# Probabilities of token tiles 4 to 7 transposed on VectorE in 32x32 blocks and moved to their rows by DMA; leftover keys on VectorE too; opening reordered

## The chip, the cores and the metric

One core of one Trainium2 chip runs the whole kernel. The metric is the device time of one launch in microseconds (us); lower is better.

## The reference, cut to what matters

One layer of a hybrid model over 1024 tokens with 16 learned meta tokens in front (L = 1040), width 1024, all in float32. One input projection feeds three mixers (a short convolution, an attention with 8 heads, a retention); their gated outputs are joined and go through an output projection that is added to the input. The change concerns the attention:

```python
cid = jnp.where(pos < 16, 0, 1 + (pos - 16) // 64)       # chunks of 64 keys, 16 meta keys in front
s = jnp.einsum('bqhd,bkhd->bhqk', qb, k) * scale         # qb: one block of 128 queries
s = jnp.where(cid_keys <= cid_queries, s, neg)
p = jax.nn.softmax(s, axis=-1)
o = jnp.einsum('bhqk,bkhd->bqhd', p, v)
o = o.reshape(B, Lp, 512) * jax.nn.silu(z)               # z: gate from the input projection ("mz")
...
h = h + y @ w_out
```

## The kernel before, in words

Matrix products keep float32 accuracy by splitting each operand in a high and a low part; `mm3` (lines 109 to 112) then issues three matmuls for one product. The kernel has three stretches.

**Opening** (0 to about 60 us). After eight warm-up matmuls, the unit `mz` of the input projection is computed from input tiles and weights that arrive by DMA. Lines 217 to 243 load the rows of x, square and sum them, and multiply a diagonal matrix on TensorE to spread the row factors (`rps`, L243). Then `rest` computes the remaining columns of `mz`, a loop over four blocks b gates and stores them (`mz_s`, L260), and unit A follows with weights `ws_A`, whose later tiles are loaded on the SP queue behind L260's stores.

**Projections, convolution and retention** (to about 345 us). Nothing of it is changed.

**Attention** (about 345 to 531 us): 8 heads of 8 token tiles t of 128 queries. A loop over n = 8h + t (lines 835 to 864) writes the work in this order: `score` of the tile that lies LA = 4 ahead, `p_t` of tile n, the transposes `qk_t` of the queries and keys of head h + 2 at tiles 3, 3, 4 and 4 (table `QK`), `attend` one tile after the last of its group of four, and `partial`, matmuls of the output projection for the mixers that are done, by a table of due tiles.
- `score` (L681 to 711): matmuls S of queries on 16 + 128(t + 1) keys into one of two PSUM slots (tile 7 needs two, S_7_0 and S_7_2); VectorE takes the row maximum (L693), ScalarE the exponential with its sum (L702) into a buffer `pr`, VectorE the reciprocal (L708); GpSimd scales the last 16 keys into `pm` (L710) and the rest in place (L711). There are 5 `pr` buffers (3 + LA - 2), taken in turn.
- `p_t` (L714 to 742): TensorE transposes `pr` in blocks of 128 keys (L724) into PSUM `pTp`, and ScalarE (L730) or, for blocks from 4 on, VectorE (L728) copies them to `pt`. The 16 leftover keys of four tiles are transposed together from `pm` (`mTp`, L736) and copied in four pieces to `ptm` (VectorE L740, ScalarE L742).
- `attend` (L744 to 773): matmuls of v on `pt` into PSUM tile `o` (L765), with the leftover keys last (L767), and two multiplications with the gate in `ym` (L773, VectorE).
- `qk_t` (L662 to 677): four transposes for 512 queries or keys (`qTp`, `kTp`), then ScalarE writes the high part, VectorE the low part.

`kTp`, `qTp` and `o` share one PSUM bank ("x"): each must be emptied before the next may start. S has two slots, `pTp` two, `part` one.

The order of instructions on each engine is fixed when the kernel is built, by a scheduler that simulates a timeline; priorities come from the order in which the code is written. At run time each engine follows its list and waits at the first instruction whose inputs are not there.

## Time and profile before

| | before |
|---|---|
| median of 3 runs | 580.92 us (580.18 to 584.61) |
| the profiled execution's own time | 581.55 us |
| span in its profile | 579.8 us |
| TensorE busy | 569.8 us, 98% |
| VectorE / ScalarE / GpSimd busy | 330.9 / 255.0 / 224.1 us |
| granted TensorE clock | 1.00 throughout (2.4 GHz) |
| chain that ended last | TensorE 83%, DMA 9%, VectorE 3% |

Each figure is one profiled execution. Busy times are sums over instructions; matmuls are pipelined, so that several of them lie over one another and a mean per matmul is longer than the time that one more of them takes. The chain of work that ended last has no such overlap: its pieces follow one another.

### The profile page before, as it was taken

Reading aid. Unit: us, or ns where it says so; the run is one execution under the profiler, and the core shown is the slowest. Engines: PE = TensorE matmul, PEld = TensorE weight load, DVE = VectorE, ACT = ScalarE, POOL = GpSimd, SP = SyncE. Lnnn points to the kernel's source line nnn. Section 1 sums busy time; section 2 is a strip of 40 time slices with the busy share of each in tenths; the row PEclk is TensorE's granted clock in tenths of the full one; section 3 lists DMA queues with packets and bytes.
Section 4 is the critical chain, followed back from the end, with each engine's and each line's share of the span. In section 5 each row is a group of like instructions: output and inputs, shape, how many; then the busy total and the mean of one; then the engine's idle time right before and its main releaser. Section 6 shows DMA issues by size and latency. Waiting matters only on the chain.

```text
span 579.8 us, 9595 instructions
## 1 busy us (share of the span) xinstructions
PE 569.8 (98%) x3401; PEld 481.7 (83%) x3401; DVE 330.9 (57%) x761; ACT 255.0 (44%) x616; POOL 224.1 (39%) x330
## 2 busy tenths in 40 slices
PE   8999999999999999999999999999999999999997
PEld 5877899988888888898898888898888888876886
DVE  5547768888536432553332667675757857664132
ACT  6765535665234332532010438475655646543000
POOL 2023258677103220151242968443524334624000
PEclk9999999999999999999999999999999999999999
DMA  8887513274703200130030648235112223113096
GB/s 326 289 265 241 182 67 120 108 224 158 234 1 92 74 0 19 54 110 18 20 97 1 199 145 273 73 103 171 56 38 73 77 71 128 37 68 116 1 301 224
DMA packets 46657, 70.39 MB, mean 121 GB/s; under 512 B 3792, under 2 KB 21840, under 8 KB 46480
## 3 DMA queue, kind: packets, MB, share of 16 engines
q1 hardware_dynamic: 43008, 63.47, 33.8%
q10 hardware_dynamic: 3600, 6.29, 2.9%
q8 instruction: 27, 0.44, 0.3%
q14 instruction: 22, 0.18, 0.1%
HBM read 48.75 MB, written 21.00 MB: 120 GB/s over the span
## 4 chain that ended last, share of the span: by engine, by line
PE 83%; DMA 9%; DVE 3%; ACT 2%; issue 2%; POOL 0%; SPq 0%; DVEq 0%; ACTq 0%; POOLq 0%
PE r L112 16%; PE S L112 9%; PE cv L112 8%; PE part L112 7%; PE A L112 6%; PE o L765 6%; PE pTp L724 5%; PE cz L112 4%; PE cb L112 4%; DMA out<-ot 4%; PE out L112 3%; PE qps L112 3%; DMA xs<-in_xT 2%; DMA xt<-in_x 2%; PE rsp L477 1%
## 5 line engine op out<-in xcount | busy, mean ns | idle before, releaser
L702 ACT ACTIVATE pr<-S,smx 128x144 f32<-128x144 f32 (+8 forms) x72 | 50.4, 701 | 27.3 <-DVE smx L693 13.4
L693 DVE TENSOR_REDUCE smx<-S 128x1 f32<-128x144 f32 (+8 forms) x72 | 49.8, 701 | 15.7 <-PE S L112 6.3
L710 POOL TENSOR_SCALAR pm<-pr,smx 128x16 f32<-128x16 f32 x64 | 18.4, 288 | 85.2 <-DVE smx L708 61.3
L711 POOL TENSOR_SCALAR pr<-pr,smx 128x128 f32<-128x128 f32 (+3 forms) x64 | 48.1, 752 | 0.6 <-DVE smx L708 0.6
L724 PE MATMUL pTp<-ident,pr 128*128 128x128 f32 x288 | 45.4, 274 | 1.5 <-ACT pt L730 1.4
L730 ACT COPY pt<-pTp 128x512 f32<-128x512 f32 (+2 forms) x64 | 31.8, 505 | 26.3 <-PE pTp L724 24.9
L451 POOL TENSOR_SCALAR kw<-qk,con 128x64 f32<-128x64 f32 (+1 forms) x36 | 13.8, 397 | 71.7 <-DVE qk L447 58.4
L724 PEld LDWEIGHTS pTp<-ident,pr 128*128 128x128 f32 x288 | 35.0, 140 | 7.0 <-POOL wol L104 1.8
L765 PEld LDWEIGHTS o<-pt,v 128*64 128x64 f32 x448 | 26.5, 137 | 12.1 <-issue 4.7
L765 PE MATMUL o<-pt,v 128*64 128x256 f32 (+2 forms) x448 | 36.2, 309 | 0.0
L112 PE MATMUL r<-wh_r,xal 128*128 128x512 f32 (+1 forms) x80 | 30.5, 381 | 0.0
L112 PE MATMUL r<-wh_r,xah 128*128 128x512 f32 (+1 forms) x80 | 30.4, 380 | 0.0
L112 PE MATMUL part<-woh,yh 128*128 128x512 f32 x64 | 30.1, 470 | 0.0
L112 PE MATMUL r<-wl_r,xah 128*128 128x512 f32 (+1 forms) x80 | 30.0, 375 | 0.0
L882 DVE SCALAR_TENSOR_TENSOR ot<-out,xr 128x512 f32<-128x512 f32 (+1 forms) x17 | 11.2, 660 | 31.1 <-DMA out<-ot 16.8
L112 PE MATMUL r<-wl_r,xbh 128*128 128x512 f32 x64 | 26.1, 409 | 0.0
L112 PE MATMUL r<-wh_r,xbh 128*128 128x512 f32 x64 | 25.7, 401 | 0.0
L112 PE MATMUL part<-wol,yh 128*128 128x512 f32 x64 | 25.5, 399 | 0.0
L112 PE MATMUL r<-wh_r,xbl 128*128 128x512 f32 x64 | 25.5, 398 | 0.0
L112 PE MATMUL part<-woh,yl 128*128 128x512 f32 x64 | 25.2, 394 | 0.0
L773 DVE TENSOR_TENSOR ym<-o,ym 64x256 f32<-64x256 f32 x32 | 13.5, 421 | 16.7 <-PE o L767 16.2
L104 POOL TENSOR_TENSOR wol<-wos,woh 128x512 fp32r<-128x512 f32 x16 | 20.4, 1291 | 2.6 <-ACT woh L103 2.6
(295 smaller groups left out, 1716.1 us busy)
## 6 DMA issues: line engine op xcount, KB each, us to landing
xt<-in_x SPq DMA_DIRECT2D x16, 256.0 KB, 4.5
ws_r<-in_win SPq DMA_DIRECT2D x16, 256.0 KB, 3.3
ws_c<-in_win SPq DMA_DIRECT2D x16, 256.0 KB, 2.9
wos<-in_wout SPq DMA_DIRECT2D x16, 256.0 KB, 3.8
xp<-in_x SPq DMA_DIRECT2D x16, 256.0 KB, 2.7
p_s<-xp SPq DMA_DIRECT2D x16, 256.0 KB, 2.0
xr<-p_s SPq DMA_DIRECT2D x15, 256.0 KB, 4.5
out<-ot ACTq DMA_DIRECT2D x15, 256.0 KB, 4.5
```

Of the source, the lines that this page charges most:

```text
L104: (lo_eng or nc.vector).tensor_tensor(lo, src, hi.bitcast(F32), op=ALU.subtract)
L112: nc.tensor.matmul(out, lhsT=x_, rhs=y_, start=first and i == 0, stop=last and i == 2)
L451: nc.gpsimd.tensor_scalar(kw[R, j], qk[R, 2 + j], con[R, kd0 + j:kd0 + j + 1], 1.0, op0=ALU.mult, op1=ALU.mult)
L693: nc.vector.tensor_reduce(sm[:, i // 2:i // 2 + 1], sp[:, :n, :w], axis=AX.XY, op=ALU.max, negate=True)
L702: e = nc.scalar.activation(pr[:, c0:c1].rearrange("p (b c) -> p b c", b=n), sp, AF.Exp, bias=mx, accum_out=sm[:, 5 + i:6 + i])
L710: nc.gpsimd.tensor_scalar(pm[(2 * h + t // 4) % 2][:, t % 4, :NM], pr[:, nk - NM:nk], sm[:, 9:10], 1.0, op0=ALU.mult, op1=ALU.mult)
L711: nc.gpsimd.tensor_scalar(pr[:, :nk - NM], pr[:, :nk - NM], sm[:, 9:10], 1.0, op0=ALU.mult, op1=ALU.mult)
L724: tr_ = nc.tensor.transpose(out=tp[:, b * P:b * P + P], in_=pr[:, c0:c0 + P], identity=ident)
L730: nc.scalar.copy(pt[:, b0:b0 + nb, tt], src)
L765: nc.tensor.matmul(op[64 * cg:64 * cg + 64, c0:c1], lhsT=lv, rhs=src[:, i_, c_], start=b == 0, stop=False)
L773: nc.vector.tensor_tensor(ys, op[64 * cg:64 * cg + 64, :256].rearrange("p (a c q) -> p a c q", a=2, q=64), ys, op=ALU.mult)
L882: nc.vector.scalar_tensor_tensor(ot, acc[:, c0:c1], 0.5, xt, op0=ALU.mult, op1=ALU.add)
```

## The change

1. **Tiles 4 to 7.** Their `pr` is no longer transposed on TensorE. VectorE transposes it within 32x32 blocks (L737 of the changed kernel) into a buffer `td`, and 16 DMAs for each pair of tiles (L746, on the SP queue, 32 partitions with rows of 352 or 480 elements) move the blocks to the partitions on which their keys belong, in `pt`. That is 32 DMAs per head, 256 in all. Tiles 0 to 3 are transposed on TensorE as before and copied by ScalarE alone.
2. **Leftover keys.** `pm` and `mTp` are gone. Two 32x32 transposes on VectorE per tile (L742) go from `pr` to `ptm`, 16 per head; GpSimd clears the end of `pr` first (L707) and normalises in one operation (L716). The rows `vr` of v for these keys are loaded for each pair of heads.
3. **attend** reads the tiles in pairs, with 40 instead of 28 matmuls on `pt` per head over the same columns, and stands 4 tiles after its group rather than 1 (`LAG`); `QK` moves from tiles (3, 3, 4, 4) to (4, 4, 5, 5). LA goes from 4 to 3, so that there are 4 `pr` buffers.
4. **Opening.** 11 warm-up matmuls, not 8; the remaining columns of `mz` are split around the row-factor matmuls and interleaved over two halves; the weight tiles 4 to 7 of unit A are loaded from within the loop over b, one per block.

```diff
-    NA, NW, GA = 4, 8, 0
+    NA, NW, GA = 4, 11, 0
...
+            if g == GA:
+                rest(2, 1, accs[2, 1], range(6))
...
+        for g in range(2):
+            r_row(g)
+        rest(2, 1, accs[2, 1], range(6, KT))
...
+        for k in range(KT):
+            for g in range(2):
+                rest(3, g, accs[3, g], (k,))
         for b in range(4):
+
+            with tc.issue_after(last_t.ins):
+                wA.append(load_w("A", len(wA)))
...
-    LA = 4
+    LA = 3
...
-    QK = (3, 3, 4, 4)
-    ON_DVE = ((4, 4), (5, 4), (6, 4), (7, 4))
-    PM_DVE = (1, 2, 3)
+    QK = (4, 4, 5, 5)
+    LAG = 4
...
+            nc.gpsimd.memset(pr[64:, nk:nk + NM], 0.0)
...
-            nc.gpsimd.tensor_scalar(pm[(2 * h + t // 4) % 2][:, t % 4, :NM], pr[:, nk - NM:nk], sm[:, 9:10], 1.0, op0=ALU.mult, op1=ALU.mult)
-            nc.gpsimd.tensor_scalar(pr[:, :nk - NM], pr[:, :nk - NM], sm[:, 9:10], 1.0, op0=ALU.mult, op1=ALU.mult)
+            nc.gpsimd.tensor_scalar(pr[:, :nk], pr[:, :nk], sm[:, 9:10], 1.0, op0=ALU.mult, op1=ALU.mult)
...
+            if t < 4:
+                tp = pst("tr", f"pTp{h}_{t}")
+                for b in range(t + 1):
+                    late["pe"] = nc.tensor.transpose(out=tp[:, b * P:b * P + P], in_=pr[:, b * P:b * P + P], identity=ident).ins
+                nc.scalar.copy(pts[h, p][:, :, d0:d0 + t + 1].rearrange("p i d q -> p d i q"),
+                               tp[:, :P * (t + 1)].rearrange("p (d i q) -> p d i q", i=4, q=32))
+            else:
+                nc.vector.transpose(tds[p][:, :, d0:d0 + t + 1].rearrange("p m d q -> p d m q"),
+                                    pr[:, :nk - NM].rearrange("p (d m k) -> p d m k", m=4, k=32))
+
+            par, r = (2 * h + t // 4) % 2, 32 * (t % 4)
+            for i in (2, 3):
+                nc.vector.transpose(late["ptm"][par][r:r + 32, t % 4, 32 * i - 64:32 * i - 32], pr[32 * i:32 * i + 32, nk - NM:nk + NM])
+            if t >= 4 and odd:
                 for i in range(4):
+                    for m in range(4):
+                        nc.sync.dma_start(pts[h, p][32 * m:32 * m + 32, i], tds[p][32 * i:32 * i + 32, m])
...
-    for n in range(len(seq) + 1):
+    for n in range(len(seq) + LAG):
...
-        if 1 <= n and seq[n - 1][1] % 4 == 3:
-            attend(seq[n - 1][0], seq[n - 1][1] // 4)
+        if n >= LAG and seq[n - LAG][1] % 4 == 3:
+            attend(seq[n - LAG][0], seq[n - LAG][1] // 4)
```

The order that the scheduler makes of it, at the places that matter below. In these rows a name with an underscore and a number is the tile of that index (`S_5` the scores of tile 5; the last number only tells generations apart), and xN says that N such instructions follow one another.

TensorE of before, in one head's attention, around the second pair of key and query transposes and the first `o` of the head:

```order
L668 MATMUL kTp_1_4090<-ident,k_3651 96x128 x4
L724 MATMUL pTp_7_0_4186<-ident,pr_7_4024 128x128 x4
...
L112 MATMUL S_5_0_4269<-kt0h,qt0l 128x392
L736 MATMUL mTp_1_4198<-ident,pm_3321 128x128
L668 MATMUL qTp_1_4097<-ident,q_3650 96x128 x4
L112 MATMUL S_6_0_4290<-kt0h,qt0h 128x456
...
L112 MATMUL part_0_4264<-woh_0_3328,yl_3962 128x512
L765 MATMUL o_0_4104<-pt_0_3932,v_3279 64x256 x2
```

TensorE of the changed kernel, at the same place of a head:

```order
L112 MATMUL S_5_0_4601<-kt1h,qt1l 128x392
L674 MATMUL kTp_1_4457<-ident,k_4245 96x128 x4
L674 MATMUL qTp_1_4464<-ident,q_4244 96x128 x4
L764 MATMUL o_0_4523<-pt_0_4238,v_3639 64x128 x2
...
L766 MATMUL o_0_4523<-ptm_3600,vr_3643 64x4x32 x2
L733 MATMUL pTp_2_4615<-ident,pr_2_4499 128x128 x3
```

The three tiles of bank x stand behind one another, where before 15 or more matmuls (S, `part`, pTp) stood between two of them.

VectorE of the changed kernel, from this place on:

```order
L107 SCALAR_TENSOR_TENSOR qt0l<-qTp_1_4464,wqk,qt0h 96x512
L742 STREAM_TRANSPOSE ptm_3600<-pr_0_4433 32x32
L771 TENSOR_TENSOR ym_3587<-o_0_4523,ym_3587 64x8x32 x2
L742 STREAM_TRANSPOSE ptm_3600<-pr_0_4433 32x32
...
L715 RECIPROCAL smx_5_4600<-smx_5_4600 128x1
L737 STREAM_TRANSPOSE td_2_4714<-pr_4_4586 128x5x4x32
L800 SCALAR_TENSOR_TENSOR xp_0_4683<-part_0_4573,xp_0_4683 128x512
L737 STREAM_TRANSPOSE td_2_4714<-pr_5_4609 128x6x4x32
L699 TENSOR_REDUCE smx_6_4625<-S_6_0_4626 128x1
L699 TENSOR_REDUCE smx_7_4691<-S_7_0_4692 128x1
```

The maximum of S_6 now stands behind the block transposes of tiles 4 and 5, and the transposes of the leftover keys behind the multiplications of `o`. Further down the same list:

```order
L704 TENSOR_REDUCE smx_7_4691<-smx_7_4691 128x1
L737 STREAM_TRANSPOSE td_3_4793<-pr_6_4634 128x7x4x32
L713 TENSOR_REDUCE smx_7_4691<-smx_7_4691 128x1
L715 RECIPROCAL smx_7_4691<-smx_7_4691 128x1
L737 STREAM_TRANSPOSE td_3_4793<-pr_7_4706 128x8x4x32
L742 STREAM_TRANSPOSE ptm_3601<-pr_4_4586 32x32
L771 TENSOR_TENSOR ym_3587<-o_1_4647,ym_3587 64x8x32 x2
...
L699 TENSOR_REDUCE smx_0_4734<-S_0_0_4735 128x1
L742 STREAM_TRANSPOSE ptm_3601<-pr_6_4634 32x32 x2
L742 STREAM_TRANSPOSE ptm_3601<-pr_7_4706 32x32 x2
```

The maximum of the next head's S_0 stands behind the block transpose of tile 7, and that behind tile 7's own normalisation. In before the list between the reciprocal of tile 7 and the maximum of the next S_0 holds, of work on probabilities, one copy for tile 4.

## Rows read from the trace of the kernel before

**Rows 1.** The page: busy us, share of the span, instructions of each engine
```profile
PE 569.8 (98%) x3401; PEld 481.7 (83%) x3401; DVE 330.9 (57%) x761; ACT 255.0 (44%) x616; POOL 224.1 (39%) x330
```

**Rows 2.** Window of one head: busy us and instructions, clock, DMA
```profile
core 0: us, PE busy (x) PEld busy (x) DVE busy (x) ACT busy (x) POOL busy (x), PEclk, DMA share, GB/s
422.00:445.60 23.60, 23.59 (x186) 19.98 (x187) 16.92 (x40) 14.10 (x35) 9.54 (x19) 1.00 0.17 57
```

**Rows 3.** Chain that ended last, one head: start us, us, what
```profile
422.00 3.03 PE o L765 x34
428.71 0.66 PE pTp L724 x6
432.91 0.70 PE part L112 x3
434.49 1.08 PE S L112 x6
440.29 1.30 PE o L765 x18
```

**Rows 4.** VectorE by line and shape, 350 to 530 us: busy us, mean ns
```profile
L773 DVE TENSOR_TENSOR ym<-o,ym 64x256 f32<-64x256 f32 x30 | 12.6, 421 | 14.7 <-PE o L767 14.2
L791 DVE SCALAR_TENSOR_TENSOR xp<-part,xp 128x512 f32<-128x512 f32 x16 | 11.0, 685 | 6.6 <-PE part L112 5.4 <-DMA vr<-v_s 0.9
L740 DVE COPY ptm<-mTp 32x64 f32<-32x64 f32 x48 | 10.7, 223 | 1.3 <-ACT ptm L742 0.4
L708 DVE RECIPROCAL smx<-smx 128x1 f32<-128x1 f32 x60 | 9.4, 157 | 8.6 <-ACT pr L702 8.1
L693 DVE TENSOR_REDUCE smx<-S 128x1 f32<-128x912 f32 x8 | 8.8, 1099 | 2.6 <-issue 2.3 <-PE S L112 0.3
L728 DVE COPY pt<-pTp 128x512 f32<-128x512 f32 x8 | 5.5, 682 | 3.3 <-PE pTp L724 3.3
L728 DVE COPY pt<-pTp 128x128 f32<-128x128 f32 x8 | 2.3, 283 | 1.5 <-PE pTp L724 1.5
L104 DVE TENSOR_TENSOR yk<-ym,yq 128x1024 fp32r<-128x1024 f32 x2 | 2.4, 1210 | 0.0
L693 DVE TENSOR_REDUCE smx<-S 128x1 f32<-128x144 f32 x7 | 2.1, 305 | 0.2
```

**Rows 5.** ScalarE by line and shape, the same stretch and columns
```profile
L702 ACT ACTIVATE pr<-S,smx 128x912 f32<-128x912 f32 x8 | 8.2, 1027 | 4.8 <-DVE smx L708 2.5 <-DVE smx L693 2.3
L702 ACT ACTIVATE pr<-S,smx 128x656 f32<-128x656 f32 x7 | 5.7, 812 | 3.8 <-ACT kt1h L103 1.9 <-ACT kt0h L103 1.9
```

**Rows 6.** GpSimd by line and shape, the same stretch and columns
```profile
L711 POOL TENSOR_SCALAR pr<-pr,smx 128x1024 f32<-128x1024 f32 x8 | 9.0, 1127 | 0.0
```

**Rows 7.** Timeline, one key tile through bank x: start us, us, engine
```profile
433.89 0.60 PE L668 MATMUL kTp<-ident,k 128*96 128x128 f32 x4
...
434.57 0.58 ACT L103 CAST kt1h<-kTp 96x512 fp32r<-96x512 f32 x1
...
435.18 0.69 DVE L104 TENSOR_TENSOR kt1l<-kTp,kt1h 96x512 fp32r<-96x512 f32 x1 [0.67 <-ACT kt1h L103]
```

**Rows 8.** Timeline of the SP queue: start us, us for xN issues
```profile
346.35 1.80 SPq L823 DMA_DIRECT2D ym<-mz_s  x4
348.19 2.92 SPq L831 DMA_DIRECT2D vr<-v_s  x5
```

**Rows 9.** DMA issues of the page: KB each, median us to landing
```profile
p_s<-xp SPq DMA_DIRECT2D x16, 256.0 KB, 2.0
```

**Rows 10.** Chain that ended last, opening: start us, us, what
```profile
53.60 3.85 DMA ws_A<-in_win
```

**Rows 11.** The same chain, end of the attention
```profile
492.70 3.03 PE o L765 x34
498.04 1.24 PE o L765 x17
531.47 18.12 PE out L112 x78
```

More of the change, by code (lines that the diff above doesn't have):

```diff
@@ L111, in mm3 @@
         for i, (x_, y_) in enumerate(((l_[0], r_[0]), (l_[0], r_[1]), (l_[1], r_[0]))):
-            nc.tensor.matmul(out, lhsT=x_, rhs=y_, start=first and i == 0, stop=last and i == 2)
+            m = nc.tensor.matmul(out, lhsT=x_, rhs=y_, start=first and i == 0, stop=last and i == 2)
+        return m.ins
     def load_w(u, k, eng=None, between=None):
@@ L177, in trunk, with rest @@
         nc.scalar.activation(acts, half_neg[:, :1], AF.Tanh)
-        def rest(b, g, a):
-            for k in range(KT):
+        def rest(b, g, a, ks=range(KT)):
+            for k in ks:
                 mm3(a, [w[:, b * P:b * P + P] for w in wmz[k]], X(k, NM + g * 512, 512), k == 0, k == KT - 1)
@@ L269, in trunk @@
     with tc.issue_after(last_t.ins):
-        wA += [load_w("A", k) for k in range(len(wA), KT)]
         nc.sync.dma_start(con, ins["con"])
@@ L647, in trunk @@
     late = {}
-    pm = [at1.tile([P, 4, 32], F32, name=f"pm{i}", bufs=1) for i in range(2)]
-    for i in range(2):
-        nc.gpsimd.memset(pm[i], 0.0)
     def pst(tag, name):
@@ L699, in score @@
                 mx = sm[:, 4:5]
[L700 removed]
+            pr = (at1 if (h * NT + t) % (LA + 1) < 3 else late["at2"]).tile([P, LQ], F32, tag="pr", name=f"pr{h}_{t}")
+            nc.gpsimd.memset(pr[64:, nk:nk + NM], 0.0)
             for i, (sp, c0, c1, n) in enumerate(chunks):
@@ L716, in p_t @@
-            if tt == 0:
-                pts[h, g] = late["ptp"].tile([P, 4 * g + 4, 4, P], F32, tag=f"pt{g}", name=f"pt{h}_{g}")
-            pt, pr = pts[h, g], prs.pop((h, t))
-            for b0 in range(0, t + 1, 4):
-                nb = min(4, t + 1 - b0)
-                tp = pst("tr", f"pTp{h}_{t}_{b0}")
-                for b in range(nb):
-                    c0 = (b0 + b) * P
-                    tr_ = nc.tensor.transpose(out=tp[:, b * P:b * P + P], in_=pr[:, c0:c0 + P], identity=ident)
-                late["pe"] = tr_.ins
-                src = tp[:, :nb * P].rearrange("p (b q) -> p b q", q=P)
-                if (t, b0) in ON_DVE:
-                    nc.vector.tensor_copy(pt[:, b0:b0 + nb, tt], src)
-                else:
-                    nc.scalar.copy(pt[:, b0:b0 + nb, tt], src)
@@ L731, in p_t @@
-            if tt == 3:
-                par = (2 * h + g) % 2
-                tp = pst("tr", f"mTp{h}_{g}")
-                nc.tensor.transpose(out=tp[:, :P], in_=pm[par].rearrange("p t m -> p (t m)"), identity=ident)
-                for i in range(4):
-                    ms = slice(32 * i, 32 * i + 32)
-                    if i in PM_DVE:
-                        nc.vector.tensor_copy(late["ptm"][par][ms, i], tp[ms, 64:P])
-                    else:
-                        nc.scalar.copy(late["ptm"][par][ms, i], tp[ms, 64:P])
+            p, odd = divmod(t, 2)
@@ new lines, in p_t @@
+            nk, d0, nd = NM + P * (t + 1), t * odd, 4 * p + 3
+            pr = prs.pop((h, t))
+            if not odd:
+                pts[h, p] = late["ptp"].tile([P, 4, nd, 32], F32, tag=f"pt{p}", name=f"pt{h}_{p}")
+                if t >= 4:
+                    tds[p] = late["ptp"].tile([P, 4, nd, 32], F32, tag=f"td{p}", name=f"td{h}_{p}")
+            if t < 4:
[7 more added lines that the diff above has]
+                                    pr[:, :nk - NM].rearrange("p (d m k) -> p d m k", m=4, k=32))
@@ new lines, in attend @@
+            op = pst("o", f"o{h}_{g}")[:, :256].rearrange("p (a t j q) -> p a t j q", a=2, t=2, j=2)
+            half = [slice(64 * cg, 64 * cg + 64) for cg in range(2)]
+            for b in range(4 * g + 4):
+                lv = vt[:, b, 64 * hh:64 * hh + 64]
+                for a in range(2):
+                    n = 2 * (2 * g + a) + 1
+                    t0 = max(0, b - n + 1)
+                    if t0 > 1:
+                        continue
+                    src = pts[h, 2 * g + a]
+                    for cg in range(2):
+                        x = src[:, cg::2, b + n * t0:b + n + 1:n].rearrange("p j t q -> p t j q")
+                        nc.tensor.matmul(op[half[cg], a, t0:], lhsT=lv, rhs=x, start=b == a == 0, stop=False)
@@ L775, in trunk, with load_rest @@
+        vrs = {}
+        def load_rest(hp):
+            vrs[hp] = late["ptp"].tile([P, 2, P], F32, tag="vr", name=f"vr{hp}", bufs=2)
+            nc.gpsimd.memset(vrs[hp], 0.0)
+            for g in range(2):
+                r0 = P * (4 * g + 1)
+                for i in range(4):
+                    nc.sync.dma_start(vrs[hp][32 * i:32 * i + NM, g], v_s[r0 + P * i:r0 + P * i + NM, P * hp:P * hp + P])
         ysp = {}
@@ L826, in trunk @@
     late["ptm"] = [late["ptp"].tile([P, 4, 64], F32, name=f"ptm{i}") for i in range(2)]
-    vr = late["ptp"].tile([P, 2, 512], F32, name="vr")
-    for x in late["ptm"] + [vr]:
+    for x in late["ptm"]:
         nc.gpsimd.memset(x, 0.0)
-    for i in range(8):
-        nc.sync.dma_start(vr[32 * (i % 4):32 * (i % 4) + NM, i // 4], v_s[P * (i + 1):P * (i + 1) + NM])
+    load_rest(0)
     late["ps2"], close_ps2 = pool("ps2", space=PSUM, side="right")
```

47 lines of the change are left out of this document (14 added, 33 removed).

## The prediction

> **What bounds the kernel now.** I read the page first: TensorE is busy 98% of the span, VectorE 57%, ScalarE and GpSimd less than half [rows 1]. Then windows of one head each, since an average hides a stage: the middle heads of the attention repeat every 23.55 us, and in such a window TensorE is busy 23.59 of 23.60 us, VectorE 16.92, ScalarE 14.10 [rows 2]. Then the chain that ended last: inside a head it consists of TensorE pieces alone, each starting where the one before ended [rows 3]. So before, every microsecond taken off TensorE's list in the attention is gained, as long as nothing else takes its place. The granted clock is 1.00 in these windows and I change nothing for it. The opening waits for DMA [rows 10], and the projections between are not touched.
>
> **The change part by part.**
>
> *TensorE.* A transpose of 128 keys costs 0.66/6 = 0.11 us of the chain [rows 3]. Of 36 pTp and 2 mTp per head 10 remain: -28 x 0.11 = -3.1 us. attend has 12 more matmuls over the same columns. A matmul of `o` takes 3.03/34 = 0.09 us at 256 columns; a narrower one more can cost nothing or at most those 0.09, so 0 to +1.1; I take +0.2, since the columns stay the same. TensorE's list falls from 23.55 to about 20.6 us per head.
>
> *VectorE, removed.* Copies of pTp, four sizes from 0.28 to 0.68 us, are 1.9 us per head; six copies of mTp at 0.22 are 1.3 us [rows 4].
>
> *VectorE, added.* No row shows a block transpose. All float32 operations of VectorE lie on one slope: the copies take (0.682 - 0.283)/384 = 1.04 ns for each further element of a partition, the maxima (1.099 - 0.305)/768 = 1.03, and 1024 elements of a subtraction 1.21 us [rows 4]. With that slope the transposes of 640, 768, 896 and 1024 elements are 0.81, 0.94, 1.08 and 1.21 us, 4.0 us per head. Lower bound half of it, upper bound twice, should the blocks cost a second pass. A 32x32 one lies between the reciprocal of one element, 0.16, and the copy of 32x64, 0.22 [rows 4]: 0.19, 16 per head are 3.0 us (2.5 to 3.6). VectorE goes from about 16.5 to 20 us per head: still below 23.55 as a sum.
>
> The Trainium skill ("VectorE: DVE Perf Modes", The three transpose paths) gives 311 ns for a 128x128 transpose in bf16 on VectorE, in 32x32 blocks, against 390 ns on TensorE, so it would call VectorE the quicker. In this kernel one on TensorE costs 0.11 us of the chain [rows 3], because they are pipelined. By the page's 311 ns the 26 block columns of a head would cost an estimated 8.1 us rather than 4.0, which is the upper bound above.
>
> *GpSimd* loses the short L710 and gains small clears; at under 10 us per head [rows 2] it is hidden, except in the chains below.
>
> *DMA.* 32 issues per head on SP. Back to back an issue takes 1.80/4 = 0.45 us, and 2.92/5 = 0.58 where the queue was full [rows 8]: 14.4 to 18.7 us per head, and 2.0 us from issue to landing [rows 9]. `o_1` of a head stands behind most of the next head's scores, so this is hidden, as long as a head lasts 20 us or more. At the end it is not.
>
> **Where a wait replaces the work.** Sums do not decide here, because each engine keeps its order. I walked one head of the changed order by hand, each step starting when its engine is free and its inputs are there.
>
> First half, from the end of tile 7's block transpose on VectorE (0) to the end of `o_0`:
> - four L742 (0.8), the two multiplications of `o_1` (0.85), maximum of S_0 (0.3): 1.95. Four L742 more, maxima of S_1 and S_2 (0.44 and 0.57 by the slope), a reciprocal, and the low part of kTp_0 (0.69): 4.7.
> - two reciprocals, the `xp` addition (0.69), maximum of S_3 (0.70): 6.4. Meanwhile qTp_0, which had to wait for kTp_0 to leave bank x, ends at 5.2; its low part on VectorE ends at 7.2.
> - on TensorE S_4 (0.9), two `part` (0.70 each), pTp_1 and S_5 (1.08) follow qTp_0 [rows 3]: 8.9.
> - now kTp_1, qTp_1 and `o_0` stand directly behind one another and share bank x. One tile through the bank takes 435.18 + 0.69 - 433.89 = 1.98 us [rows 7]: 10.9, and qTp_1, with its longer scaled split, 13.0. `o_0`, 1.30 to 1.5 [rows 3]: **14.4**. In before other matmuls fill these four microseconds.
>
> Second half, from the end of `o_0` (0) to the end of the next block transpose of tile 7:
> - VectorE: L742, two multiplications, L742: 1.25. Only now is `pr` of tile 0 read, and with 4 buffers that is the buffer which the exponential of S_4 needs. Exponentials of S_4 (0.81) and S_5 (0.93), sums, reciprocal: 3.5 [rows 4, 5]. Behind this reciprocal in VectorE's list stand block transposes of tiles 4 and 5 with an `xp` between (0.81 + 0.69 + 0.94): 6.0.
> - maximum of S_6, which stands behind them (1.1): 7.1. Its exponential (1.03) frees the slot for S_7_2: 8.2. Six matmuls' half (0.5), its maximum (0.51) and the joining one: 9.4.
> - exponentials of S_7 (0.84 and 0.54 with their sums), adding, reciprocal: 11.3. GpSimd normalises tile 7 (1.13) [rows 6]: 12.5. Its block transpose (1.21) ends at **13.6**, and the next half begins, since the multiplications of `o_1` and the next maximum of S_0 stand behind it.
>
> Together 28.0 us against 23.55. Nothing fills TensorE meanwhile, because its own next instructions are S, kTp or o that wait for exactly these steps. Heads with this order are four of the five periods in the middle. In the fifth `o_1` stands ahead of S_7_2, and the same walk gives 23.4. Mean 27.1: +3.5 for each of five.
>
> The rest of the sum. Start: the first head has LA = 3 and its `o_0` stands four tiles later; +2 (0 to 3.5, one period's loss). The last two heads have no transposes of queries and keys, and took 531.47 - 492.70 = 38.8 us from `o_1` of one to the output stage [rows 11]; second half 13.6 and a first half of about 7 each, 41.2: +2.4. End: the last tile pair's 16 DMAs can be issued only after its block transpose, 16 x 0.45 + 2.0 = 9.2 us in place of eight pTp (0.9) and a copy (0.7), -1.6; of these 7.6 about 2.6 are covered by `part` and `o_0`: +5. Opening: the last weights of A came 3.85 us after their issue, late in the list [rows 10]; loading them within the loop, and warming up longer, can bring 0 to 3.5: -2, since SP still has the gate's stores to issue before them.
>
> Sum: 5 x 3.5 + 2 + 2.4 + 5 - 2 = +24.9. With the profiled execution's 581.55: 606.4. The median of the runs lies 0.6 below it: **606**.
>
> **The rivals.**
> 1. *TensorE stays the bound* (faster). Then 8 x -2.95 - 2 = -25.6 and 556. It decides when a head's two halves take under 23.55 together. That needs 4.5 us less than I walked, more than the block transposes that stand in the chain cost (0.81 + 0.94 + 1.21 = 3.0). For it speaks that the head has no other work that is this long; against it, that kTp_1, qTp_1 and `o_0` stay in a row. 0.10.
> 2. *VectorE's busy time is the bound* (faster). 20 us of work plus a tenth of waiting is 22 per head: -1.55 x 8 - 2 + 5 at the end = -9.4, 572. It needs the exponentials and GpSimd's steps to hide under VectorE's work, which its order does not do for tile 7. 0.09.
> 3. *The block transposes cost half* (2.0 per head; 1.5 of it on the chain) and the leftover ones little (2 less on the chain): 24.5 per period, 5 x 0.95 + 2 + 5 - 3 = +9 and 590. No row of VectorE has this price. 0.12.
> 4. *They cost twice* (the upper bound): +3.0 in each of five periods and twice 2.9 more in the last heads, 626. 0.12.
> The forecast itself has 0.57, with 592 to 622 as its own range: the leftover transposes' bounds give about 4 us either way, start, end and opening 10 together.
>
> **How the numbers follow.** About 1% (6 us) is what a measurement of this kernel can tell from no change. Rivals 1 and 2 give faster, 0.19. The lower part of 3, below 587, is within 1%, 0.06. All else is slower, 0.75. Low 574 leaves out rival 1 and half of 2; high 625 leaves out half of 4: 0.2 in all.
>
> **What the profile after would show.** TensorE's transposes L733 near 80 instead of 288 pTp, and its busy share in windows of a head falling to about 20.6 of 27 to 28 us. In the chain of waits, VectorE, ScalarE and GpSimd should appear inside a head, with L737, L742 and L716 ahead of S_7 and S_0; and TensorE idle before qTp_1 and `o_0`, released by the low-part splits on VectorE. L737 should show 0.81 to 1.21 us by shape, L742 about 0.19. At the end, TensorE should wait some 5 us or more for the last L746. I am wrong if the period of a head is below 23.55, which TensorE busy in the whole window would show; or if L737 and L742 are far from these prices.

## The result, and the profile after

The changed kernel is slower, and by more than the range allowed: 642.17 us against 580.55, a ratio of 1.108 (95% interval 1.104 to 1.112). The ratio is taken over executions in the chip's faster state alone, so it differs a little from the quotient of the medians. The forecast was 606 us, and at most 625.

| | before | after |
|---|---|---|
| median | 580.55 us | 642.17 us |
| span of the profiled execution | 579.8 us | 643.3 us |
| first score of the attention (S) starts | 331.2 | 332.8 |
| `o_1` of head 0 ends | 376.0 | 391.5 |
| `o_1` of head 5 ends | 495.9 | 538.6 |
| output stage starts | 531.5 | 595.3 |

So 1.6 us lie ahead of the attention (scatter: in the profiled executions of the other kernels with this opening, e14 aside, the first S starts between 329.5 and 333.3), 13.9 are lost in its beginning, 27.2 in the five middle periods (29.4 us each instead of 24.0) and 21.1 in the last two heads. The output stage takes 48 us as before.

The page of after, same columns as [rows 1], and the granted clock in 40 slices (9 is full speed, 2.4 GHz):

```profile
PE 577.1 (90%) x3372; PEld 483.9 (75%) x3372; DVE 362.8 (56%) x841; ACT 239.2 (37%) x568; POOL 214.9 (33%) x331
...
PEclk9998999999999999999999898797989879985999
```

TensorE has fallen from 98 to 90%, but no other engine has come near its place: VectorE is at 56% of a longer span. Nothing is full, so things wait. Windows from one end of `o_1` to the next, in after (columns as in [rows 2]):

```profile
419.20:452.80 33.60, 25.61 (x182) 21.17 (x181) 21.40 (x50) 11.21 (x27) 9.80 (x21) 0.85 0.53 147
452.80:479.70 26.90, 23.90 (x179) 19.51 (x178) 19.18 (x46) 10.68 (x24) 7.38 (x18) 0.87 0.41 114
...
567.50:595.30 27.80, 9.00 (x90) 7.52 (x90) 4.01 (x14) 0.00 (x0) 1.60 (x2) 0.63 0.31 81
```

VectorE's work per head is about 20 us, as forecast. The clock column is the surprise: 0.85 and 0.87 in the two middle heads, where it was 1.00 in [rows 2], and in the last window TensorE works 9 of 27.8 us at 0.63. VectorE by line and shape, as in [rows 4]:

```profile
L742 DVE STREAM_TRANSPOSE ptm<-pr 32x32 f32<-32x32 f32 x122 | 24.8, 204 | 18.6 <-PE o L766 15.3 <-POOL pr L716 0.6
...
L737 DVE STREAM_TRANSPOSE td<-pr 128x1024 f32<-128x1024 f32 x8 | 9.9, 1237 | 4.0 <-POOL pr L716 4.0
...
L737 DVE STREAM_TRANSPOSE td<-pr 128x640 f32<-128x640 f32 x8 | 6.7, 838 | 2.4 <-POOL pr L716 2.2 <-DMA pt<-td 0.2
```

The prices were right. What TensorE waited for from 370 to 600 us in after (us in total, times, longest):

```profile
PE o L764 <- DMA pt<-td: 24.9, 8, 8.1
PE S L112 <- ACT pr L709: 7.5, 6, 2.4
PE o L764 <- DVE qt1l L107: 4.7, 3, 1.6
```

The largest sum is for the new DMAs, but they do not hold every head: 3.5 of the 24.9 us lie in head 0, 17.6 in front of and within `o_1` of the last head, and only 3.8 in the five middle periods. There most of the idle time is waiting for bank x, above all at the place that the prediction named, `kTp_1`, `qTp_1` and `o_0` in a row. TensorE of after there (idle time before it in brackets):

```profile
431.53 0.64 PE L674 MATMUL qTp<-ident,q 128*96 128x128 f32 x4 [1.39 <-DVE kt0l L104]
433.73 1.89 PE L764 MATMUL o<-pt,v 128*64 128x128 f32 x24 [1.56 <-DVE qt0l L107]
```

The same pair of waits, 2.9 us together, stands in four of the five periods, as the walk had it. All waits for bank x are 15.3 of the 24.7 us that TensorE idles in the five.

SP's queue in after (start us, us for xN issues):

```profile
452.06 20.90 SPq L746 DMA_DIRECT2D pt<-td  x32
...
566.77 21.38 SPq L746 DMA_DIRECT2D pt<-td  x32
```

32 issues take 20.90 us, 0.65 each; a batch begins 0.2 to 0.8 us ahead of the end of `o_1` of the head before. The chain that ended last, at the end of the attention in after (start us, us, what), shows how they close a loop:

```profile
564.50 2.25 PE o L764 x40
566.77 0.51 SPq L746
...
586.93 0.59 SPq L746
587.56 2.03 DMA pt<-td
589.59 0.24 issue
589.84 5.09 PE o L764 x45
```

`o_1` of head 6 reads `pt` of tiles 4 to 7; there is one such buffer, so the issues for head 7 begin when it has been read (566.77); the last lands at 589.6, and `o_1` of head 7 runs, slowed by the clock (5.09 us from 589.84, the granted clock 0.55 from 589.8 to 595.3; at 416.2 the same 45 matmuls took 2.66 us at 1.00). That is 28 us in which TensorE works 9.

The 3.8 us in the middle lie in one head, and something stands in the queue there that the prediction did not price: the loads of `vr` for the next pair of heads, which part 2 of the change put into the attention. SP's queue in after, at that head:

```profile
419.03 1.15 SPq L746 DMA_DIRECT2D pt<-td  x2
...
420.91 6.27 SPq L782 DMA_DIRECT2D vr<-v_s  x8
```

The other 30 issues begin at 427.22, 7 us behind the first two, and the period takes 33.6 us. That the loads are the cause is read from the queue; no run moves them.

### The profile page after: what moved, and what is told of

Same layout as the page of the kernel before. It is cut to its first block, busy times and chain, and to the rows that moved or that the text cites. A ratio compares the mean times of both kernels' runs of the same rounds, so it can differ in the third digit from the quotient of the medians.

```text
span 643.3 us, 9969 instructions
## 1 busy us (share of the span) xinstructions
PE 577.1 (90%) x3372; PEld 483.9 (75%) x3372; DVE 362.8 (56%) x841; ACT 239.2 (37%) x568; POOL 214.9 (33%) x331
## 4 chain that ended last, share of the span: by engine, by line
PE 66%; DMA 11%; SPq 10%; DVE 7%; ACT 3%; issue 3%; POOL 1%; DVEq 0%; ACTq 0%; POOLq 0%
PE r L112 15%; SPq L746 9%; PE cv L112 7%; PE A L112 6%; PE o L764 6%; PE S L112 4%; PE part L112 4%; PE cz L112 3%; PE cb L112 3%; PE out L112 3%; PE qps L112 3%; DMA out<-ot 3%; DMA xs<-in_xT 2%; DVE smx L699 2%; DMA xt<-in_x 1%
## 5 line engine op out<-in xcount | busy, mean ns | idle before, releaser
L764 PE MATMUL o<-pt,v 128*64 128x128 f32 (+1 forms) x640 | 51.2, 311 | 33.6 <-DMA pt<-td 24.9
L764 PEld LDWEIGHTS o<-pt,v 128*64 128x64 f32 x640 | 44.4, 166 | 44.5 <-issue 36.9
L716 POOL TENSOR_SCALAR pr<-pr,smx 128x144 f32<-128x144 f32 (+3 forms) x64 | 48.4, 759 | 58.3 <-DVE smx L715 51.4
L737 DVE STREAM_TRANSPOSE td<-pr 128x640 f32<-128x640 f32 (+3 forms) x32 | 33.1, 1038 | 9.6 <-POOL pr L716 7.7
L742 DVE STREAM_TRANSPOSE ptm<-pr 32x32 f32<-32x32 f32 x128 | 26.1, 204 | 18.7 <-PE o L766 15.3
L707 POOL MEMSET pr<- 64x16 f32 x64 | 6.7, 106 | 77.4 <-DVE ptm L742 73.3
L890 DVE SCALAR_TENSOR_TENSOR ot<-out,xr 128x512 f32<-128x512 f32 (+1 forms) x17 | 11.2, 660 | 30.8 <-PE out L112 14.5
L112 PE MATMUL part<-wol,yh 128*128 128x512 f32 x64 | 27.5, 430 | 0.0
L112 PE MATMUL part<-woh,yl 128*128 128x512 f32 x64 | 27.3, 426 | 0.0
L112 PE MATMUL S<-kt1h,qt1h 104*128 104x348 f32 (+7 forms) x56 | 20.8, 371 | 5.3 <-ACT pr L709 5.3
L112 PE MATMUL S<-kt0h,qt0h 104*128 104x348 f32 (+7 forms) x56 | 20.2, 360 | 2.7 <-ACT pr L709 2.6
```

Source lines behind the costliest of these rows:

```text
L112: m = nc.tensor.matmul(out, lhsT=x_, rhs=y_, start=first and i == 0, stop=last and i == 2)
L707: nc.gpsimd.memset(pr[64:, nk:nk + NM], 0.0)
L716: nc.gpsimd.tensor_scalar(pr[:, :nk], pr[:, :nk], sm[:, 9:10], 1.0, op0=ALU.mult, op1=ALU.mult)
L737: nc.vector.transpose(tds[p][:, :, d0:d0 + t + 1].rearrange("p m d q -> p d m q"), pr[:, :nk - NM].rearrange("p (d m k) -> p d m k", m=4, ...
L742: nc.vector.transpose(late["ptm"][par][r:r + 32, t % 4, 32 * i - 64:32 * i - 32], pr[32 * i:32 * i + 32, nk - NM:nk + NM])
L764: nc.tensor.matmul(op[half[cg], a, t0:], lhsT=lv, rhs=x, start=b == a == 0, stop=False)
```

## The experiments

The kernels without the DMAs to `pt` (e1, e6, e7, e9, e13 to e15, e18) compute `o` from values at wrong places or from constants, with the same matmuls in number and shape. Ratios are against the kernel before, run beside them. For each kernel the scheduler makes its order anew, so a difference between two kernels holds the part that was left out and the order that came of it; where the order differs at a place that matters, I say so.

**e4: the opening alone** (before, with item 4 of the change).

> The kernel before with the changed opening alone (11 warm-up matmuls, split and interleaved rest, loads of A's weights within the loop). My prediction: 2 us faster (0 to 3.5). By the trace of after: 1.2 us gained up to the first A matmul, but 1.6 us lost at the first S, since A's fourth weight tile still goes out behind the gate's stores (54.25 against 53.60 us): ratio 1.001 to 1.004.

580.02 us, ratio 0.9999 (0.9984 to 1.0014). The opening does nothing. In after A's first matmul starts at 53.7 us rather than 54.9, but A's fourth weight tile still leaves SP at 54.25, behind the gate's stores, and TensorE waits 2.9 us for it.

**e1: without the DMAs.** A tile pair's DMAs are left out and attend reads `td`.

```diff
-                for i in range(4):
-                    for m in range(4):
-                        nc.sync.dma_start(pts[h, p][32 * m:32 * m + 32, i], tds[p][32 * i:32 * i + 32, m])
+                pts[h, p] = tds[p]
```

> The changed kernel without its 256 DMAs from td to pt: attend reads the block-transposed td itself, so its matmuls are the same in number and shape, over values at wrong places (the output is not the reference's). Theory D: the period of a head is set by the DMAs. SP issues 32 of them per head at 0.63 us (20.3 us), they may start only when o_1 of the head before has read pt, land 2 us later, and o_1 takes 3 to 4 us more: a loop of 26 to 27 us, and the waits of o on pt<-td (24.9 us in the trace of after) go. Then this kernel falls to at most 595 us. Theory V: the chain of VectorE, ScalarE and GpSimd that I walked (28 us per head) sets the period and the DMAs lie in its gaps: 632 us or more. Both in turn (one ends last in some heads, the other in others): 605 to 622 us.

613.34 us, ratio 1.057 (1.055 to 1.059): both theories in turn, by the traces the DMAs at the beginning and the end and VectorE in between. The DMAs, with the order that goes with them, are worth 29 us, the rest 33. The period in the middle is 28.0 us (the last four matmuls of `o_0` of successive heads start at 430.59, 458.71 and 486.55), the number that I walked for four of the five heads, but in another order: here 21 matmuls stand between `kTp_1` and `qTp_1` and none between `kTp_0` and `qTp_0`. The chain of one head in e1:

```profile
468.72 0.63 PE kTp L674 x4
469.35 1.30 DVE smx L699 x2
470.64 0.03 issue
470.67 1.11 DVE td L738
...
473.01 1.07 PE qTp L674 x4
...
474.99 1.37 PE part L112 x3
...
478.89 0.70 PE part L112 x3
```

TensorE idles for 3.7 us, until VectorE, behind two maxima, a block transpose and two leftover ones, has emptied bank x:

```profile
473.00 1.09 PE L674 MATMUL qTp<-ident,q 128*96 128x128 f32 x4 [3.67 <-DVE smx L704]
```

Then the same three `part` matmuls take 1.37 us, and 0.70 again at 478.89. Windows of e1 over that place:

```profile
469.40:473.00 3.60, 0.00 (x1) 0.01 (x1) 3.51 (x7) 0.55 (x1) 0.19 (x3) 0.78 0.11 28
473.00:478.90 5.90, 5.90 (x20) 4.88 (x21) 3.49 (x10) 2.85 (x8) 1.60 (x3) 0.56 0.00 0
478.90:486.50 7.60, 7.38 (x62) 6.28 (x63) 5.38 (x10) 3.67 (x11) 3.06 (x4) 1.00 0.31 104
```

After the idle stretch the granted clock is 0.56, so mostly the lower level, 1.2 GHz, for 5.9 us. How much of a period is waiting and how much the clock shows over the five middle heads of e1, of after and of e15 (below, without either kind of transpose), with practically the same matmuls in each (columns as in [rows 2]):

```profile
381.70:521.60 139.90, 118.27 (x902) 98.05 (x901) 104.35 (x248) 57.53 (x137) 42.78 (x97) 0.89 0.24 74
391.50:538.60 147.10, 122.44 (x902) 100.58 (x901) 101.50 (x246) 58.56 (x138) 41.70 (x95) 0.88 0.45 124
378.30:484.40 106.10, 102.31 (x901) 88.97 (x901) 66.89 (x147) 58.78 (x138) 43.88 (x97) 1.00 0.32 99
```

TensorE idles 21.6 us in e1, 24.7 in after and 3.8 in e15, and at the lower clock its matmuls are busy 16 and 20 us longer than in e15. Of the 21.6, 18.2 are the one wait above, five times.

**e12: the price of an issue.** DMAs behind the end of the kernel before, on an empty queue.

```diff
...
+    for i in range(4):
+        for m in range(4):
+            nc.sync.dma_start(c[0][32 * m:32 * m + 32, i], a[32 * i:32 * i + 32, m])
+    for m in range(4):
+        nc.sync.dma_start(c[1][:, m], a[:, m])
...
```

> The kernel before with DMAs added behind its end, on an idle SP queue, to measure the price of an issue by itself: 16 from 32 partitions to 32 others (1920 B rows, as in the change), 4 from 128 partitions to the same 128, 8 from 32 partitions to the same 32, 4 to DRAM from 128 partitions, and 4 back. If the shape makes the 0.63 us per issue (32 rows that change partitions): the first group 0.55 to 0.65 each, the 128-partition ones 0.33 to 0.45. If a busy queue made it: all of them 0.33 to 0.47 us. Its own time is not compared.

Neither. SP's queue in that stretch (start us, us for xN issues; L909 32 partitions to 32 others, L911 128 to the same 128, L914 32 to the same 32, all within SBUF; L916 to DRAM, L918 back):

```profile
580.53 10.10 SPq L909 DMA_DIRECT2D pc<-pa  x16
590.68 2.53 SPq L911 DMA_DIRECT2D pc<-pa  x4
593.25 5.04 SPq L914 DMA_DIRECT2D pc<-pa  x8
598.33 2.05 SPq L916 DMA_DIRECT2D pd<-pa  x4
```

0.63 us apart whether 32 or 128 partitions and whether they change partitions or not; to DRAM 0.51. The issues alone take 0.589, 0.600, 0.588 and 0.448 us in the median, and 0.320 from DRAM (L918, not in the rows). Of what was varied, only the two memories of the transfer changed the price. They are not all of it: in e5 the median issue is 0.35 us from SBUF to DRAM and 0.42 back. The issues in [rows 8] load from DRAM.

**e2 and e5: fewer issues on SP.** e2 issues every second DMA on ScalarE's queue. e5 goes through DRAM with 5 issues per pair.

```diff
-                        nc.sync.dma_start(pts[h, p][32 * m:32 * m + 32, i], tds[p][32 * i:32 * i + 32, m])
+                        (nc.sync, nc.scalar)[m % 2].dma_start(pts[h, p][32 * m:32 * m + 32, i], tds[p][32 * i:32 * i + 32, m])
...
+                nc.sync.dma_start(scr, tds[p].rearrange("p m d q -> p m (d q)"))
+                for m in range(4):
+                    nc.sync.dma_start(pts[h, p][32 * m:32 * m + 32].rearrange("p i d q -> p i (d q)"),
+                                      scr[:, m].rearrange("(i p) x -> p i x", p=32))
```

> The changed kernel with the DMAs from td to pt issued half on SP's and half on ScalarE's queue (m even, m odd). Theory D: SP's part of a head falls from 20.3 to 10.2 us and the wait of o on pt<-td shrinks to little: 610 to 622 us. Theory V: unchanged or worse, since ScalarE, which stands in the chain, must issue 16 DMAs of 0.6 us per head: 642 to 660 us.

> The changed kernel with each tile pair's move from td to pt in 5 DMAs rather than 16: one writes td to a scratch in DRAM, four read it back to the 32 partitions they belong on; 10 per head in place of 32, all the bytes twice. If the number of issues on SP makes the waits of o on pt<-td (theory D, issues): about 6 us of issues per head in place of 20, the waits go although each move now takes two landings: 611 to 622 us, near the 613 of the kernel without these DMAs. If it is the bytes or the time to landing (theory D, transfer): no better, 636 to 655 us.

e2: 637.12 us, ratio 1.099 (1.097 to 1.101); e5: 630.79, 1.087 (1.081 to 1.094). Both fall short of what theory D gave them. In e2 TensorE still waits 12.1 us for `pt<-td`, all of it in the last two heads, and ScalarE, which is in the chain, now stands behind issues of its own: its exponentials wait 14.1 us for these DMAs. In e5 the waits of `o` on the DMA are 3.2 us between 400 and 500 us, but 28.7 in the whole attention, and the way over DRAM costs 17 us more than none (e1). It loses them where nothing lies behind the DMAs to cover them: its five middle heads take 139.1 us (139.9 in e1), the beginning up to `o_1` of head 0 is 6 us longer than in e1 and the last two heads 9.7, with 19 us of these waits. So fewer issues help, up to 11 of the 29 us; whether the rest is the two landings or the order built around them, I did not separate.

**e3: tiles 4 to 7 on TensorE again**, everything else as changed.

> The changed kernel with tiles 4 to 7 transposed on TensorE again (copied by ScalarE, blocks from 4 on by VectorE), everything else as changed: LA 3, LAG 4, QK, the leftover keys on VectorE, attend by pairs, the opening. No td, no DMA to pt. If the block transposes and their DMAs are all that costs time, TensorE is the bound again with 26 transposes more than the change (2.9 us per head): 578 to 586 us. If the order (kTp_1, qTp_1 and o_0 in a row on one bank, L742 ahead of the maxima, 4 buffers) costs by itself, as I walked it with the block transposes at nothing (24.4 us per head against 23.55): 588 to 605 us.

591.53 us, ratio 1.019 (1.017 to 1.021). What is left of the change without the block transposes and their DMAs costs 11 us.

**e6, e7, e8: what I named in the order.** e6 and e8 put `o` in the two banks of pTp (e6 on e1, e8 on e3); e7 has LA = 4, five `pr` buffers, on e1.

```diff
-        if tag == "tr" or "ps2" not in late:
+        if tag in ("tr", "o") or "ps2" not in late:
...
-    LA = 3
+    LA = 4
```

> The kernel without the DMAs (e1, 613 us, 28.0 us per head as walked), with the tiles o moved from bank x to the two banks of pTp. By my walk the first half ends with S_5 at 8.9, kTp_1 2.0, qTp_1 2.05 and o_0 1.4 in a row, because they share bank x. With o elsewhere, o_0 need not wait for qTp_1 (-2.05 us per head) nor, should it move ahead of both in the list, for kTp_1 (-4.1): about 7 periods, so 584 to 600 us. If the shared bank is not what holds the head: 608 to 615 us.

> The kernel without the DMAs with LA = 4 again, so that there are five pr buffers as before (they fit without pt of tiles 4 to 7). By my walk the exponential of S_4 waits for pr of tile 0 to be read by L742, 1.25 us behind o_0, and all of the second half (13.6 us) starts from there; with a fifth buffer the exponentials of S_4 and S_5 can run before o_0: 2 to 3 us less per head, 592 to 602 us. If the buffers do not hold the head: 608 to 617 us.

> The changed kernel with tiles 4 to 7 transposed on TensorE (e3, 591.5 us, 24.85 us per head), with the tiles o in the two banks of pTp in place of bank x. If the 1.3 us per head that e3 loses against before come from bank x (kTp_1, qTp_1, o_0 in a row): 579 to 585 us, TensorE busy throughout a head. If they come from the other parts of the order (four pr buffers, L742 on VectorE): 588 to 593 us.

607.72 us (ratio 1.047, 1.043 to 1.050), 605.70 (1.043, 1.040 to 1.047) and 587.50 (1.013, 1.009 to 1.018). Each brings 4 to 8 us, less than my walk promised: neither of the two alone holds a head. In the five middle heads of e1 TensorE waits 18.2 us for `qTp` behind `kTp` in bank x and 0.9 us in front of S for the exponentials; in e6, which moves `o` alone, 8.2 and 8.8; in e7 0.3 and 8.5, and 7.8 for `qTp` in front of `o`. One wait gives way to another. And the row that the walk blamed, `kTp_1`, `qTp_1`, `o_0`, does not stand in e1, so e6 does not show what bank x costs in after; that was not tested. In e8 four of the five middle heads last about 23.8 us each and the fifth 22.3 (the five of before: 24.0 in the mean), so what e8 still loses lies in the first and the last two heads.

**e9 and e10: the clock.** Behind each head's key transposes, matmuls whose results nobody reads (16 behind kTp_0, 4 behind kTp_1), on e1 and on after.

```diff
...
+                with tc.issue_after(tr_.ins):
+                    for _ in range((16, 4)[g] if which else 0):
+                        nc.tensor.matmul(fill[:, :512], lhsT=ident.bitcast(BF16)[:, :P], rhs=wo_fill.bitcast(BF16), start=True, stop=True)
```

> The kernel without the DMAs (e1, 613 us; granted clock 0.88 in a head) with 16 matmuls of 512 columns, whose results nobody reads, behind each head's kTp_0 and 4 behind kTp_1, where TensorE sat idle for 3.7 us until qTp_0 could start. In e1 the matmuls behind that idle time run at half speed for about 5.9 us (three part matmuls take 1.28 to 1.37 us, not 0.70). If the clock costs what these rows say, half of 5.9, so 2.9 us per head over five or six heads: 594 to 600 us. If the clock hides behind VectorE's chain anyway: 608 to 616 us.

> The changed kernel (642 us, granted clock 0.85 in the attention) with the same filling matmuls behind the key transposes. If part of the loss of the changed kernel is the clock alone, and the idle place is the same as in e1: 622 to 634 us. But TensorE also idles there in front of o, for the DMAs, where nothing is filled in; if the clock falls there and that is what costs: 636 to 645 us.

e9: 605.45 us, 7.9 less than e1; mean clock from 360 to 560 us 0.97, against 0.89 in e1 (360 to 563). e10: 637.61, 4.6 less than after; 0.93 against 0.85. In e9 the clock costs about half of what I read from the rows: with the clock restored the period is still 26.3 us, which fits VectorE's chain being the later one in part of that stretch. e10 does not tell what the clock costs in after: its five middle heads, at a clock of 0.98 and with some 4 us of filling matmuls each, take 146.6 us (147.1 in after); the gain lies ahead of the attention and in the last two heads, where no filling matmul stands.

**e11: the leftover keys alone**, in the kernel before.

```diff
-            nc.gpsimd.tensor_scalar(pm[(2 * h + t // 4) % 2][:, t % 4, :NM], pr[:, nk - NM:nk], sm[:, 9:10], 1.0, op0=ALU.mult, op1=ALU.mult)
...
+            for i in (2, 3):
+                nc.vector.transpose(late["ptm"][par][r:r + 32, tt, 32 * i - 64:32 * i - 32], pr[32 * i:32 * i + 32, nk - NM:nk + NM])
```

> The kernel before with one part of the change alone: the leftover keys transposed on VectorE (16 transposes of 32x32 per head from pr to ptm, pr's end cleared and normalised in one operation on GpSimd), no pm, no mTp. LA, LAG, QK, the transposes of all tiles on TensorE and the opening as before. TensorE's list loses two mTp of 0.11 us per head, VectorE gains 16 x 0.204 - 6 x 0.22 = 1.9 us per head and stays at 19 of 23.5. If TensorE stays the bound: 578 to 580 us, ratio 0.995 to 0.999. If the transposes on VectorE hold up maxima and copies as in the changed kernel: 583 to 590 us.

589.83 us, ratio 1.014 (1.011 to 1.018). This small part costs 9 us, although it takes work off TensorE. A head lasts 24.7 us.

**e13, e14, e15: leaving out, on e1**, the block transposes (e13), the leftover transposes (e14), and both (e15).

> The kernel without the DMAs (e1, 613 us) and without the 32 block transposes of tiles 4 to 7 as well: attend reads two constant tiles in their place. By my walk 0.84 + 0.96 of tiles 4 and 5 and 1.24 of tile 7 lie on the chain, 3.0 us of a head, some 7 heads: 590 to 595 us, which is also where e3 came out (591.5 us). If they lie beside other work of VectorE, or the order around them holds the head: 602 us or more.

> The kernel without the DMAs (e1, 613 us) and without the 128 transposes of the leftover keys: ptm stays constant. 16 of them per head at 0.204 us are 3.3 us of VectorE. If all of them stand on the chain: 613 - 8 x 3.3 = 587 us. If they cost what they cost in the kernel before (e11, 8.6 us): 604 us. By my walk ten of 16 stand on it (2.0 us a head): 597 to 600 us.

> The kernel without the DMAs, without the block transposes and without the transposes of the leftover keys: only the order, four pr buffers, the lag of attend, the shorter list of TensorE and the opening are left of the change. If these transposes are the whole of what is left, TensorE is the bound with its list 2.9 us per head shorter: 581 - 8 x 2.9 + 2 = 560 us (557 to 565). If the changed order closes a chain by itself, as I walked it (24.4 us per head): 580 to 592 us.

| without the DMAs | leftover transposes | without them |
|---|---|---|
| **block transposes** | 613.3 (e1) | 600.2 (e14) |
| **without them** | 590.1 (e13) | 560.6 (e15) |

Ratios: e13 1.016 (1.012 to 1.021), e14 1.034 (1.031 to 1.036), e15 0.967 (0.964 to 0.970). e15 is the gain that the change is after: TensorE's shorter list, bound by TensorE, 21.2 us per head. A window over two heads:

```profile
414.40:456.80 42.40, 40.89 (x364) 35.55 (x360) 26.98 (x59) 23.44 (x56) 17.25 (x40) 1.00 0.25 77
```

So the lag and the new places of the key transposes cost nothing by themselves. For after's own order that is not shown: in e15 15 matmuls stand between `kTp_0` and `qTp_0`, and 6 between `kTp_1`, `qTp_1` and `o_0` each, which stand in a row in after. Each kind of transpose alone takes the gain away (30 us for the leftover keys, 40 for the blocks); together they cost 53, less than the sum, which fits their lying in part in the same waits. A transpose that is left out also reads no `pr`, whose buffer comes free earlier; the differences hold that too. The chain of e13 shows how 3.3 us of VectorE can cost 30 us over eight heads:

```profile
428.33 0.27 PE o L762 x4
428.61 0.05 issue
428.66 0.20 DVE ptm L740
...
431.90 0.52 DVE smx L699
...
433.29 0.94 ACT pr L709 x2
434.23 0.04 issue
434.28 0.92 PE S L112 x3
435.19 1.37 PE part L112 x3
```

`o_1` ends at 428.6; six leftover transposes and two multiplications stand behind it on VectorE, with the maxima of S_7 among and behind them, and only then the low part of the keys, which empties bank x. In these 5.7 us TensorE works 3.75 and waits for that bank:

```profile
433.19 1.01 PE L674 MATMUL qTp<-ident,q 128*96 128x128 f32 x4 [1.88 <-DVE smx L704]
```

Behind that it runs at the lower clock (1.37 us for three `part`). Over the five middle heads of e13 it idles 14.8 us and its matmuls are busy 112.5; in e15 3.8 and 102.3.

**e18: four ptm buffers.** The leftover transposes of tiles 4 to 7 stand there because `ptm` has two buffers, and the one they write was last read by `o_1`. e13 with four:

```diff
-    late["ptm"] = [late["ptp"].tile([P, 4, 64], F32, name=f"ptm{i}") for i in range(2)]
+    late["ptm"] = [late["ptp"].tile([P, 4, 64], F32, name=f"ptm{i}") for i in range(4)]
...
-            par, r = (2 * h + t // 4) % 2, 32 * (t % 4)
+            par, r = (2 * h + t // 4) % 4, 32 * (t % 4)
```

> The kernel of e13 (590 us: no DMAs, no block transposes, the leftover keys on VectorE) with four ptm buffers in place of two. With two, the leftover transposes of tiles 4 to 7 must wait until o_1 of the head before has read the same buffer, so that they stand in a row behind o_1 on VectorE, ahead of the maxima of S_7 and S_0; with four, they stand spread over the head, each behind its tile's normalisation. If it was this place that cost 30 us (590 against 560.6 of e15, which leaves these transposes out): 560 to 568 us, although VectorE does the same work. If it was the work (16 x 0.204 = 3.3 us per head) or the buffers pr that they keep: 582 to 592 us.

570.87 us, ratio 0.982 (0.979 to 0.987). The same work on VectorE, 19 of the 30 us back, though 3 us above the range that the place alone was to give. It was mainly the place, together with the order that TensorE gets by it: in a middle head e18 has the order of e15, where e13 has `kTp_0` and `qTp_0` in a row. VectorE's list now has each tile's two transposes behind its own normalisation, spread over the head, which is 21.95 us long at clock 1.00. The 10 us that are left I did not separate into the work and the `pr` buffers that it keeps.

**e16 and e17: a smaller form.** Tiles 4 and 5 alone (e16) or 6 and 7 alone (e17) by VectorE and DMA, the leftover keys through `pm` and `mTp` as before, LA = 4.

> A smaller form of the change: block transposes and DMAs for tiles 4 and 5 alone (16 DMAs per head), tiles 6 and 7 on TensorE again, the leftover keys through pm and mTp as before, five pr buffers (LA 4); opening, LAG and QK as changed. TensorE's list loses 11 transposes of 0.11 us per head, 1.2 us; VectorE gains 1.8 us of block transposes and loses the two smaller copies, 0.7. If the chain through the leftover transposes and the fourth-buffer wait was what let VectorE hold the head, TensorE stays the bound: 572 to 578 us. If two block transposes and a DMA loop of 10 us are enough to hold it: 583 to 600 us.

> The same with tiles 6 and 7 in place of 4 and 5: 15 transposes less on TensorE, 1.65 us per head; VectorE gains 2.35 us. The block transpose of tile 7 stands behind tile 7's whole chain and 16 DMAs follow it, at the end of the attention with nothing to hide them. If TensorE stays the bound but for the end (16 x 0.63 + 2 = 12 us there in place of 1.6): 572 to 584 us. If the chain through tile 7 holds the head: 588 to 605 us.

592.18 us (1.019, 1.014 to 1.023) and 599.74 (1.032, 1.027 to 1.036). Neither beats before. In e17 `o` waits 10.8 us for `pt<-td`, 8.0 of it in one wait near the end; in e16 the longest sum is 6.5 us for the low part of qTp. No complete kernel here is faster than before.

## Why the prediction was right or wrong

What the parts were to cost, and what they cost, in us against before (after and e1 from their profiled executions):

| | forecast | after | e1, without the DMAs |
|---|---|---|---|
| ahead of the attention | -2 | +1.6 | +0.4 |
| beginning, to the end of `o_1` of head 0 | +2 | +13.9 | +5.3 |
| five middle periods | +17.5 | +27.2 | +20.0 |
| last two heads, to the output stage | +7.4 | +21.1 | +6.6 |

- **Direction and bound: right.** Slower was forecast. TensorE does not stay the bound, and with rival 1's premise made true (e15) the time is 560.6, where that rival had 556. TensorE's list is 20.5 us of e15's 21.2 per head, forecast 20.6.
- **VectorE's prices: right.** Block transposes 0.84 to 1.24 us (forecast 0.81 to 1.21), leftover ones 0.204 (0.19), 20 us of VectorE per head. The 26 block columns of a head took 33.1/8 = 4.1 us. Rival 4, at twice the price, falls. The Trainium skill ("VectorE: DVE Perf Modes", The three transpose paths) gives 311 ns for one 128x128 transpose in bf16. Taken once for each block column it would have made 8.1, and the trace does not agree with that; but the line through the four shapes has, by an estimate, 0.838 - 512 x 0.00104 = 0.31 us at 128 columns, so the figure fits one instruction of 128 columns, and a wider one pays the fixed part only once.
- **DMA: wrong, and the largest miss.** Two steps failed. "Back to back an issue takes 0.45 us" came from loads out of DRAM; moves within SBUF are 0.63 us apart (e12), which the upper end of 0.58 did not cover either. And "hidden, as long as a head lasts 20 us or more" overlooked that `pt` of these tiles has one buffer: the issues cannot start before `o_1` of the head before has read it. 32 x 0.65 + 2.0 + 3 to 5 for `o_1` is a loop of 26 to 28 us. It costs 29 us by the medians (e1), 31.5 in the profiled executions of the table: 9.8 of it up to `o_1` of head 0, 7.2 in the five middle heads, where e1 loses 20 of its own, and 14.5 in the last two heads. The end was priced with the last 16 DMAs; all 32 lie on the path. The loads of `vr`, which hold the queue 6.3 us in one middle head, were in no term. The Trainium skill ("DMA: Bandwidth & Descriptors", Rules for kernel authors) wants transfers under 64 KB coalesced, being mostly overhead. These are 44 and 60 KB, and the trace agrees: 60 KB landed in 2.0 us and 240 KB in 2.4, at the same issue price (e12).
- **The clock: wrong.** "I change nothing for it." TensorE's waits bring the lower clock with them: 0.85 from 360 to 595 us. In the five middle heads the matmuls of after are busy 20 us longer than the same ones in e15, those of e1 16 us. Not all of it is lost time: filling one idle place of e1 gave back 7.9 us (e9). For after the price stays open (e10).
- **The walk: the place right, the size by luck.** That TensorE would idle in front of `qTp_1` and `o_0` in four of the five middle periods came true in after, with 2.9 us each time. The walk had 28.0 us for those four, 23.4 for the fifth, 27.1 in the mean; after took 29.4, and e1 28.0. That e1 has the walked number is luck: its order is another, all five of its heads take 27.4 to 29.0, and some 3 us of each are the clock, which the walk did not have. The moved bank and the fifth buffer are worth 6 and 8 us on e1 (e6, e7), where I had put 14 to 28 and 11 to 21 ahead of those runs. What the walk had on its chain of the transposes themselves came out: 23 us in all for the block ones (3.0 per head walked; e1 against e13) and 13 for the leftover ones (2.0 per head; e14). With the block ones gone the leftover ones are worth 30 (e13, e15), because of where they stand and the order that comes of it (e18).
- **Start and opening: wrong.** The start's +2 was +13.9, of which the DMAs are 8.6; the opening's -2 was 0 (e4).

Summed from 580.6: -20 for TensorE's shorter list (e15), +53 for the two kinds of transposes and what their waits do to the clock (e1), +29 for the DMAs. These are differences between kernels with orders of their own. They show which parts cost the time; how much of each is the part and how much the order that came with it stays open.

## What to carry to other kernels

Before work is moved off a full engine, look for what the receiving engine must wait for: a short operation that waits for a buffer's last reader holds everything queued behind it, so count buffers along the new path (here `ptm` and `pt`) before counting microseconds of work. Price an issue of DMA from a row with the same two memories, and ask when the first of a batch may start, not only how long the batch is. When a change makes TensorE wait, look at the matmuls behind the wait at the lower clock too. And when variants are compared, look first at whether the scheduler gave them the same order.
